# Attention on one core: the running maximum folded from 128 to 64 partitions ahead of its transposes

## The chip, the cores and the metric

The kernel runs on one core of a Trainium2 chip. A core has a matrix engine (TensorE, PE in the profile, with its weight loads as PEld), three engines for elementwise work (VectorE or DVE, ScalarE or ACT, GpSimd or POOL), and SyncE (SP), whose queue issues most of the transfers. Each engine works through its own list of instructions in order; between engines they wait for each other on semaphores. The metric is device time in microseconds for one execution of the whole layer.

## The reference, cut to what matters

One encoder layer with two groups of token mixers side by side: gated linear attention (group A) and multi-head latent attention (group B). Their outputs are concatenated, go through one output projection, and a LayerNorm of the scaled residual follows. The change touches the attention of group B alone:

```python
def attend(blk):
    qn, qr = blk
    s = (jnp.einsum('bqhd,bkhd->bhqk', qn, k_nope, preferred_element_type=jnp.float32)
         + jnp.einsum('bqhr,bkr->bhqk', qr, k_r, preferred_element_type=jnp.float32))
    p = jax.nn.softmax(s, axis=-1)
    return jnp.einsum('bhqk,bkhv->bqhv', p.astype(v.dtype), v)
```

There are 4 heads and 2048 positions; a softmax runs over all 2048 keys. It needs, for each query, the maximum of its scores over the keys, which is subtracted ahead of the exponential.

## The kernel before, in words

The kernel runs group A first, then the projections of group B, then from about 620 us on the attention, and last the output projection with its LayerNorm. Products are made to full precision by splitting each operand into a high and a low part, so one product is three matmuls (the helper at lines 419 to 423).

The attention (from line 1488) works in 16 blocks: 4 heads by 4 groups of 512 queries. Scores are held with **keys on the partitions and queries along the columns**. A block has 8 pairs of key tiles; a pair is 2 x 128 keys, and its scores fill a tile of 128 x 1024. For a pair, TensorE makes the scores (ten matmuls, tile pS, lines 1522 to 1526); ScalarE copies them to SBUF (s, line 1531); VectorE folds them into the running maximum (rm, 128 x 512, lines 1541 and 1544); later VectorE subtracts the block's maximum (line 1568), ScalarE takes the exponential (line 1572) and rounds its high part (ph, line 367), GpSimd takes the low part (pl, line 373), and TensorE multiplies by the values (o, six matmuls, lines 421 to 423). Sums of the exponentials run beside it: VectorE adds some pairs into ap (line 1595), GpSimd others into acc (lines 1598 and 1600).

After the last pair, rm still holds 128 partial maxima for each query, one on each partition. The kernel brings them together in three steps. In `tmax` TensorE transposes rm in four pieces of 128 columns into one PSUM bank (mx, line 1550). In `rmax` VectorE reduces each piece along its columns (mc, 128 x 4, line 1555). In `bmax` TensorE transposes each column of mc, spread over 128 columns, so that the maximum of each query stands on all partitions (mb, line 1562). Only then can the first subtraction of the block start.

The sums of the exponentials go a similar way at the block's end, in a form that the change takes up: ScalarE copies one half of the partitions onto the other (`own_half`, line 1627), VectorE adds the two halves (`fold`, line 1633), TensorE transposes two pieces instead of four (sx, line 1645), and VectorE reduces them over 256 columns (line 1654). Tiles mx, sx and the projected output y share one PSUM bank (tag x); y leaves it by a ScalarE copy (yc, line 1696).

The order of all engines is written out by hand. Each step gets a place, a number in units of one pair (tables `PLACE` from line 74, `PLACE_LAST` for the last block); all steps are sorted by it (line 1768) and every engine is held to that order (`in_order`, line 383):

```python
for i in range(nb):
    for j in range(NP):
        t = NP * i + j
        put(t, scores, i, j)
        ...
    for n, f in (("tmax", tmax), ("rmax", rmax), ("bmax", bmax)) + {nb - 1: (), nb - 2: own_late}.get(i, own):
        put(NP * i + NP - 1 + at(n, i), f, i)
```

So pair j of block i has place 8i + j for its scores, and a step of the table is counted from there; tmax, rmax and bmax are counted from the block's last pair, 8i + 7. The value products of pair 4 have 12.27 (`pv`), those of block i - 1 thus 8i + 8.27, or 1.27 when counted from block i's last pair. The running adds of line 1595, the sum's copies and folds, and the output steps are placed by the same tables.

Of the kernel before, what the change touches and what calls it, by code (L numbers as in the profile page):

```python
# [9 lines left out]
F32 = mybir.dt.float32  # L10
F32R = mybir.dt.float32r
I32 = mybir.dt.int32
AF = mybir.ActivationFunctionType
ALU = mybir.AluOpType
AX = mybir.AxisListType
# [3 lines left out]
P = 128  # L19
# [8 lines left out]
QB = 512  # L28
# [45 lines left out]
PLACE = dict(  # L74
    copy=0.73,
    max=1.21,
    sub=(9.47, 8.65, 7.39, 7.37, 7.49, 6.63, 6.95, 7.44),
    exp=(10.18, 9.95, 7.63, 9.15, 8.26, 9.12, 7.84, 8.01),
    hi=(10.39, 10.41, 9.81, 10.32, 9.82, 10.74, 10.53, 10.47),
    lo=(11.99, 11.22, 11.21, 12.62, 11.98, 11.51, 10.87, 10.63),  # L80
    pv=(12.35, 12.1, 11.89, 12.65, 12.27, 12.25, 12.14, 11.45),
    acc=(12.45, 11.78, 12.32, 0, 10.57, 11.24, 10.03, 9.22),
    acc0=10.78,
    tmax=1.26,
    rmax=1.27,
    bmax=1.48,
    tot=11.2,
    half=11.7,
    fold=11.95,
# [5 lines left out]
    y=16.55,  # L95
    yc=16.9,
)
PLACE_LAST = dict(
    sub=(9.67, 8.74, 8.38, 6.77, 10.45, 3.53, 9.53, 5.55),
    exp=(10.14, 9.35, 10.49, 8.31, 13.01, 14.59, 17.1, 18.05),  # L100
    hi=(10.43, 11.83, 12.21, 14.39, 15.18, 22.96, 28.7, 34.03),
# [255 lines left out]
class K:  # L357
# [1130 lines left out]
    def attention(self):  # L1488
        tc, nc = self.tc, self.nc
        mm = nc.tensor.matmul  # L1490
        V, G, Ac = nc.vector, nc.gpsimd, nc.scalar
        NP = NKT // 2
        with ExitStack() as ctx:
# [4 lines left out]
            pM, pO, pX, pA, pS = bank("pM"), bank("pO"), bank("pX"), bank("pA"), bank("pS", 2)  # L1498
            blocks = [(h, b) for b in range(NQB) for h in range(H)]
            nb = len(blocks)  # L1500
            stt = [dict(s=[None] * NP) for _ in blocks]
# [31 lines left out]
            def smax(i, j):  # L1533
# [8 lines left out]
                else:  # L1542
                    for e in range(2):
                        V.tensor_tensor(d["rm"], src[:, e], d["rm"], ALU.max)  # L1544

            def tmax(i):
                d = stt[i]
                d["x"] = pX.tile([P, 4, P], F32, tag="x", name=f"mx{i}")
                for e in range(4):
                    nc.tensor.transpose(d["x"][:, e], d["rm"][:, e * P:(e + 1) * P], self.ident)  # L1550

            def rmax(i):
                d = stt[i]
                d["mc"] = op.sm.tile([P, 4], F32, tag="mc", name=f"mc{i}")
                V.tensor_reduce(d["mc"], d["x"], AX.X, ALU.max)

            def bmax(i):

# [53 lines left out]
            def tot(i):  # L1612
# [4 lines left out]
                    return  # L1617
                for e in range(2):
                    V.tensor_tensor(d["ap"], d["ap"], d["as"][:, e], ALU.add)

            halves = [(slice(64 * e, 64 * e + 64), slice(64 - 64 * e, 128 - 64 * e), slice(e * QB // 2, (e + 1) * QB // 2))
                      for e in range(2)]

            def own_half(i):
                d = stt[i]
# [88 lines left out]
            def put(place, fn, *a):  # L1714
                todo.append((place, len(todo), fn, a))

            def at(f, i, j=None):
                p = PLACE_LAST.get(f, PLACE[f]) if i == nb - 1 else PLACE[f]
                return p[j] if isinstance(p, tuple) else p

            own = (("tot", tot), ("half", own_half), ("fold", fold), ("tsum", tsum), ("rcp", rcp), ("keep", keep), ("oh", oh), ("ol", ol), ("y", y), ("yc", yc))
            own_late = tuple(e for e in own if e[1] is not keep)
# [4 lines that stand above are left out]
                    for n, f in (("copy", copy), ("max", smax), ("sub", sub), ("exp", exp), ("hi", phi), ("lo", plo),  # L1727
                                 ("pv", pv), ("acc", acc)):
                        if n != "acc" or j != SUM_POOL[0] or i == nb - 1:
                            put(t + at(n, i, j), f, i, j)  # L1730
                put(NP * i + at("acc0", i), acc0, i)
                for n, f in (("tmax", tmax), ("rmax", rmax), ("bmax", bmax)) + {nb - 1: (), nb - 2: own_late}.get(i, own):
                    put(NP * i + NP - 1 + at(n, i), f, i)
                if i + 2 < nb:
                    put(NP * i + 4.05, fetch, i + 2)
# [295 lines left out]
```

## Time and profile before

| what | value |
|---|---|
| median of 3 runs | 1301.71 us (1299.26 to 1301.95) |
| profiled execution, own time | 1305.11 us |
| its span, first to last instruction | 1303.1 us |
| mean granted clock of TensorE | 0.997 |

In the profile's rows an engine is named by its letters, L and a number is a line of the kernel before, and "out<-in" names the tiles. A row of a timeline gives the start in us from the span's start, the duration, engine, line, operation and shapes; "x2" stands for two instructions that follow one another, and a bracket at the end gives the idle time of that engine just before, with what ended it. The ends of matmuls are modelled, and two matmuls overlap in the rows, so TensorE's pace is read from starts.

### The profile page before, as it was taken

What the parts mean: (1) busy time and instruction counts of PE and PEld (TensorE: products, weight loads), DVE (VectorE), ACT (ScalarE), POOL (GpSimd) and SP (SyncE); (2) the same over time, 40 slices, a digit from 0 to 9 for tenths busy, and PEclk for the clock granted to TensorE, in tenths of its full rate; (3) what the DMA queues carried; (4) which work ended last, traced back from release to release, by engine and by line L of the source; (5) the groups of instructions that cost most, each with busy time, mean ns of one, the idle gap of its engine ahead of it and who ended that gap; (6) DMA issues with size and microseconds to landing.
All of it is one profiled execution on the core that took longest, in us unless ns stands there. A gap on an engine that the chain in (4) does not pass through costs nothing.

```text
span 1303.1 us, 20008 instructions
## 1 busy us (share of the span) xinstructions
PE 1276.8 (98%) x7051; PEld 1126.2 (86%) x7051; DVE 970.7 (74%) x1742; ACT 821.2 (63%) x1369; POOL 783.8 (60%) x494
## 2 busy tenths in 40 slices
PE   7999999999999999999999999999999999999997
PEld 7999999999989999999788888888888887887886
DVE  7967774645675445555798888888888889486998
ACT  7764656655575565665688888888888888511110
POOL 0143333242448666672188888889999999934441
PEclk9999999999999999999999999999999999999999
DMA  8132313122475565555501111122223110375563
GB/s 285 62 101 54 94 49 91 56 68 79 131 241 170 190 216 192 179 193 170 163 1 41 41 41 41 41 57 60 63 78 100 43 41 9 122 237 169 198 199 111
DMA packets 107820, 145.82 MB, mean 112 GB/s; under 512 B 17250, under 2 KB 62694, under 8 KB 107720
## 3 DMA queue, kind: packets, MB, share of 16 engines
q1 hardware_dynamic: 99128, 142.41, 35.1%
q0 software_dynamic: 672, 2.10, 0.4%
q8 instruction: 56, 0.92, 0.3%
q10 hardware_dynamic: 7920, 0.03, 0.3%
q14 instruction: 44, 0.36, 0.1%
HBM read 94.14 MB, written 50.36 MB: 111 GB/s over the span
## 4 chain that ended last, share of the span: by engine, by line
PE 82%; DVE 4%; DMA 4%; ACT 3%; POOL 2%; issue 1%; SPq 0%; DVEq 0%; ACTq 0%; POOLq 0%
PE o L421 4%; PE o L422 4%; PE o L423 4%; PE pS L1522 4%; PE pS L1524 4%; PE pS L1523 4%; PE pS L1525 4%; PE pS L1526 4%; PE ipa L421 4%; PE ipa L423 4%; PE ipa L422 4%; PE pz L422 2%; PE pz L423 2%; PE pz L421 2%; PE ipg L421 2%; PE ipg L422 2%
## 5 line engine op out<-in xcount | busy, mean ns | idle before, releaser
L373 POOL TENSOR_TENSOR pl<-s,ph 128x1024 fp32r<-128x1024 f32 x128 | 306.1, 2414 | 55.8 <-ACT ph L367 55.8
L1544 DVE TENSOR_TENSOR rm<-pS,rm 128x512 f32<-128x512 f32 x210 | 144.8, 690 | 26.3 <-ACT s L1531 20.7
L1568 DVE TENSOR_TENSOR s<-s,mb 128x1024 f32<-128x1024 f32 x128 | 151.2, 1213 | 9.0 <-PE mb L1562 8.9
L1531 ACT ACTIVATE s<-pS 128x1024 f32<-128x1024 f32 x128 | 131.3, 1026 | 37.4 <-PE pS L1526 33.0
L1031 POOL TENSOR_TENSOR Us<-Us,cw 128x512 f32<-128x512 f32 x16 | 18.5, 1157 | 226.5 <-DVE Us L1029 174.7
L367 ACT ACTIVATE ph<-s 128x1024 fp32r<-128x1024 f32 x128 | 135.2, 1058 | 15.8 <-PE o L423 15.0
L1572 ACT ACTIVATE s<-s 128x1024 f32<-128x1024 f32 x128 | 131.5, 1051 | 13.4 <-DVE s L1568 13.3
L421 PE MATMUL ipa<-wah,xah 128*128 128x384 f32 (+1 forms) x384 | 130.5, 340 | 6.3 <-ACT wah L367 6.2
L422 PE MATMUL ipa<-wal,xah 128*128 128x384 f32 (+1 forms) x384 | 124.8, 325 | 0.1
L423 PE MATMUL ipa<-wah,xal 128*128 128x384 f32 (+1 forms) x384 | 124.9, 325 | 0.0
L1522 PE MATMUL pS<-qh,ckvT_h 128*128 128x512 f32 x256 | 102.6, 401 | 0.8 <-DVE rm L1544 0.4
L421 PE MATMUL o<-ph,vh 128*128 128x512 f32 x256 | 101.0, 395 | 0.0
L1525 PE MATMUL pS<-rh,krs 128*128 128x512 f32 x256 | 99.8, 390 | 0.0
L1523 PE MATMUL pS<-ql,ckvT_h 128*128 128x512 f32 x256 | 99.8, 390 | 0.0
L1524 PE MATMUL pS<-qh,ckvT_l 128*128 128x512 f32 x256 | 99.8, 390 | 0.0
L423 PE MATMUL o<-ph,vl 128*128 128x512 f32 x256 | 99.8, 390 | 0.0
L1526 PE MATMUL pS<-rl,krs 128*128 128x512 f32 x256 | 99.8, 390 | 0.0
L422 PE MATMUL o<-pl,vh 128*128 128x512 f32 x256 | 99.6, 389 | 0.0
L1595 DVE TENSOR_TENSOR ap<-ap,s 128x512 f32<-128x512 f32 x120 | 83.1, 693 | 3.5 <-ACT s L1572 0.7
L373 POOL TENSOR_TENSOR ol<-of,oh 128x512 fp32r<-128x512 f32 x32 | 42.9, 1343 | 66.2 <-ACT oh L367 65.4
L421 PEld LDWEIGHTS ipa<-wah,xah 128*128 128x128 f32 x384 | 73.2, 191 | 7.4 <-ACT wah L367 6.5
L421 PE MATMUL pz<-xch,wzh 128*128 128x256 f32 x256 | 74.8, 292 | 0.0
(327 smaller groups left out, 3874.7 us busy)
## 6 DMA issues: line engine op xcount, KB each, us to landing
xcf<-xT_dram SPq DMA_DIRECT2D x16, 512.0 KB, 5.2
xr<-x_dram SPq DMA_DIRECT2D x16, 512.0 KB, 6.3
out_dram<-rr SPq DMA_DIRECT2D x32, 256.0 KB, 2.1
xaf<-xT_dram SPq DMA_DIRECT2D x14, 512.0 KB, 4.3
oib<-oi_s SPq DMA_DIRECT2D x16, 256.0 KB, 4.2
qdb<-qd_s SPq DMA_DIRECT2D x16, 256.0 KB, 4.1
SU<-su_s SPq DMA_DIRECT2D x16, 256.0 KB, 4.5
ub<-u_s SPq DMA_DIRECT2D x16, 256.0 KB, 4.4
```

The source lines that it names most:

```text
L367: return nc.scalar.activation(dst, src, AF.Copy).ins
L373: return e.tensor_tensor(dst, src, hi.bitcast(F32), ALU.subtract).ins
L421: mm(out, ah, bh, start=start, stop=False)
L422: mm(out, ah, bl, start=False, stop=False)
L423: mm(out, al, bh, start=False, stop=stop)
L1522: mm(ps[:, e], kh, qh, start=True, stop=False)
L1523: mm(ps[:, e], kh, ql, start=False, stop=False)
L1524: mm(ps[:, e], kl, qh, start=False, stop=False)
L1525: mm(ps[:, e], kr, rh, start=False, stop=False)
L1526: mm(ps[:, e], kr, rl, start=False, stop=True)
L1544: V.tensor_tensor(d["rm"], src[:, e], d["rm"], ALU.max)
L1568: V.tensor_tensor(s, s, d["mb"][:, None, :].to_broadcast([P, 2, QB]), ALU.subtract)
```

## The change

In fourteen of the sixteen blocks (all but the first and the last), two steps come ahead of the transposes. In `other_half` ScalarE copies, for each half of the partitions, 256 columns of rm from the other half into the mx bank (two copies of 64 x 256, from SBUF to PSUM). In `fold_max` VectorE takes the maximum of these and the half's own 256 columns (two instructions of 64 x 256). After that the lower 64 partitions hold queries 0 to 255 and the upper 64 hold queries 256 to 511, each with 64 partial maxima, in 128 x 256. So `tmax` transposes two pieces instead of four, and `rmax` reduces 256 columns instead of 512, over 64 at a time. `bmax` is as before.

The places of the three old steps move in these blocks: tmax from 1.26 to 1.55, rmax from 1.27 to 1.56, bmax from 1.48 to 1.78. The new steps are at 1.22 and 1.23. The first and the last block keep the old steps and places.

```diff
@@ PLACE
-    tmax=1.26,
-    rmax=1.27,
-    bmax=1.48,
+    hmax=1.22,
+    fmax=1.23,
+    tmax=1.55,
+    rmax=1.56,
+    bmax=1.78,
...
+PLACE_FIRST = dict(
+    tmax=1.26,
+    rmax=1.27,
+    bmax=1.48,
+)
 PLACE_LAST = dict(
+    tmax=1.26,
+    rmax=1.27,
+    bmax=1.48,
...
+            halves = [(slice(64 * e, 64 * e + 64), slice(64 - 64 * e, 128 - 64 * e), slice(e * QB // 2, (e + 1) * QB // 2))
+                      for e in range(2)]
+
+            folded = lambda i: 0 < i < nb - 1
+
+            def other_half(i):
+                d = stt[i]
+                d["x"] = pX.tile([P, 4, P], F32, tag="x", name=f"mx{i}")
+                f = d["x"][:, 2:4].rearrange("p a t -> p (a t)")
+                for own_p, other_p, qs in halves:
+                    Ac.activation(f[own_p], d["rm"][other_p, qs], AF.Copy)
+
+            def fold_max(i):
+                d = stt[i]
+                f = d["x"][:, 2:4].rearrange("p a t -> p (a t)")
+                for own_p, _, qs in halves:
+                    V.tensor_tensor(d["rm"][own_p, :QB // 2], f[own_p], d["rm"][own_p, qs], ALU.max)
+
             def tmax(i):
                 d = stt[i]
-                d["x"] = pX.tile([P, 4, P], F32, tag="x", name=f"mx{i}")
-                for e in range(4):
+                if not folded(i):
+                    d["x"] = pX.tile([P, 4, P], F32, tag="x", name=f"mx{i}")
+                for e in range(2 if folded(i) else 4):
                     nc.tensor.transpose(d["x"][:, e], d["rm"][:, e * P:(e + 1) * P], self.ident)
 
             def rmax(i):
                 d = stt[i]
                 d["mc"] = op.sm.tile([P, 4], F32, tag="mc", name=f"mc{i}")
-                V.tensor_reduce(d["mc"], d["x"], AX.X, ALU.max)
+                if not folded(i):
+                    V.tensor_reduce(d["mc"], d["x"], AX.X, ALU.max)
+                else:
+                    V.tensor_reduce(d["mc"].rearrange("p (e j) -> p j e", e=2),
+                                    d["x"][:, 0:2].rearrange("p j (e k) -> p j e k", e=2), AX.X, ALU.max)
...
-                p = PLACE_LAST.get(f, PLACE[f]) if i == nb - 1 else PLACE[f]
+                p = PLACE_LAST.get(f, PLACE[f]) if i == nb - 1 else PLACE_FIRST.get(f, PLACE[f]) if i == 0 else PLACE[f]
...
-                for n, f in (("tmax", tmax), ("rmax", rmax), ("bmax", bmax)) + {nb - 1: (), nb - 2: own_late}.get(i, own):
+                fmax = (("hmax", other_half), ("fmax", fold_max)) if folded(i) else ()
+                for n, f in fmax + (("tmax", tmax), ("rmax", rmax), ("bmax", bmax)) + {nb - 1: (), nb - 2: own_late}.get(i, own):
                     put(NP * i + NP - 1 + at(n, i), f, i)
```

More of the change, by code (lines that the diff above doesn't have):

```diff
@@ L1619, in tot @@
                     V.tensor_tensor(d["ap"], d["ap"], d["as"][:, e], ALU.add)
-            halves = [(slice(64 * e, 64 * e + 64), slice(64 - 64 * e, 128 - 64 * e), slice(e * QB // 2, (e + 1) * QB // 2))
-                      for e in range(2)]
             def own_half(i):
```

## The prediction

> **What bounds the kernel now.** I read the page first (shares of busy time, the granted clock, the chain of waits), then the windows of the attention stage, its list of waits, and the timeline around one block boundary.
>
> ```profile
> PE 1276.8 (98%) x7051; PEld 1126.2 (86%) x7051; DVE 970.7 (74%) x1742; ACT 821.2 (63%) x1369; POOL 783.8 (60%) x494
> ...
> PEclk9999999999999999999999999999999999999999
> ...
> PE 82%; DVE 4%; DMA 4%; ACT 3%; POOL 2%; issue 1%; SPq 0%; DVEq 0%; ACTq 0%; POOLq 0%
> ```
>
> TensorE carries 82% of the chain that ends last, at a full granted clock. The change lies in the attention stage, from about 640 to 1098 us. Busy time in two windows, the second well inside that stage:
>
> ```profile
> 635.00:645.00 10.00, 8.91 (x43) 6.87 (x41) 8.43 (x12) 5.07 (x5) 0.00 (x0) 1.00 0.33 93
> 700.00:900.00 200.00, 200.00 (x914) 165.31 (x913) 179.87 (x250) 169.03 (x191) 169.41 (x72) 1.00 0.18 46
> ```
>
> PE (the first figure after the width) is busy 200.00 of 200 us; VectorE (third), ScalarE (fourth) and GpSimd (fifth) have 20 to 31 us free. From the list of waits of 640 to 1098 us (in total, times, longest):
>
> ```profile
> DVE mc L1555 <- PE mx L1550: 10.6, 14, 0.9
> PE mb L1562 <- DVE mc L1555: 0.8, 1, 0.8
> ```
>
> Today VectorE waits for the transposes of the maximum (14 times, 10.6 us together), and TensorE waits for the maximum only once, 0.8 us. So TensorE's own list sets the pace: a matmul taken from it is a gain, an idle gap in it is a loss, one for one. Boundary of block 3, TensorE's timeline (start, duration, instruction):
>
> ```profile
> 725.08 0.39 PE L1522 MATMUL pS<-qh,ckvT_h 128*128 128x512 f32 x1
> ...
> 727.12 0.39 PE L1526 MATMUL pS<-rl,krs 128*128 128x512 f32 x1
> 727.35 0.60 PE L1550 MATMUL mx<-ident,rm 128*128 128x128 f32 x4
> 727.70 0.48 PE L421 MATMUL o<-ph,vh 128*128 128x512 f32 x1
> 728.02 0.39 PE L422 MATMUL o<-pl,vh 128*128 128x512 f32 x1
> ...
> 729.16 0.60 PE L1562 MATMUL mb<-ident,mc 128*128 128x128 f32 x4
> 729.52 0.48 PE L1522 MATMUL pS<-qh,ckvT_h 128*128 128x512 f32 x1
> 729.83 0.39 PE L1523 MATMUL pS<-ql,ckvT_h 128*128 128x512 f32 x1
> ```
>
> Starts, not durations, tell the pace: nine steps from 725.08 to 727.12 are 0.227 us each. A group of four transposes takes 0.35 us to the next start, and that next matmul takes 0.32 instead of 0.227: 728.02 - 727.35 - 0.227 = 0.44 us for the mx group, and from 729.16 to 729.83 likewise 0.44 for mb. Both: 0.89 us a block. Between the two groups stand six matmuls of the probabilities by the values, and under them VectorE reduces the maximum:
>
> ```profile
> 724.36 1.42 DVE L1544 TENSOR_TENSOR rm<-pS,rm 128x512 f32<-128x512 f32 x2 [0.85 <-ACT s L1531]
> 725.69 1.42 DVE L1595 TENSOR_TENSOR ap<-ap,s 128x512 f32<-128x512 f32 x2
> 727.98 0.69 DVE L1555 TENSOR_REDUCE mc<-mx 128x4 f32<-128x512 f32 x1 [0.87 <-PE mx L1550]
> ...
> 729.87 3.48 DVE L1568 TENSOR_TENSOR s<-s,mb 128x1024 f32<-128x1024 f32 x3 [0.57 <-PE mb L1562]
> ```
>
> The reduction ends at 728.67 and mb goes at 729.16: 0.5 us to spare. **That cover is what the change moves.**
>
> **The change part by part.** *1. The order on TensorE.* tmax goes from place 1.26 to 1.55 and bmax from 1.48 to 1.78. The six o matmuls of pair 4 of the block before have place 1.27 on the same scale: they stood between mx and mb, and now stand ahead of mx. The changed list reads: ten score matmuls, six o matmuls, two mx, four mb, next scores. Nothing lies between mx and mb any more, so TensorE waits there through the whole reduction. Block 0 of this very trace has that order already, having no earlier block to fill the gap:
>
> ```profile
> 638.59 0.66 PE L1550 MATMUL mx<-ident,rm 128*128 128x128 f32 x4 [0.31 <-DVE rm L1544]
> 639.28 0.69 DVE L1555 TENSOR_REDUCE mc<-mx 128x4 f32<-128x512 f32 x1 [0.75 <-DMA rh<-rh_s]
> 640.03 0.65 PE L1562 MATMUL mb<-ident,mc 128*128 128x128 f32 x4 [0.79 <-DVE mc L1555]
> 640.43 0.48 PE L1522 MATMUL pS<-qh,ckvT_h 128*128 128x512 f32 x1
> 640.75 0.39 PE L1523 MATMUL pS<-ql,ckvT_h 128*128 128x512 f32 x1
> ```
>
> Four legs: first mx to reduction 0.69 (0.63 at block 3, where TensorE came in running); reduction 0.69; its end to mb 0.06; mb to the second score matmul 0.72.
>
> *2. What is cheaper.* Two mx transposes fewer, at 0.35 / 4 = 0.0875 us each: the first leg is 0.63 - 0.175 = 0.455 us. The reduction has 256 columns instead of 512. These group rows of the stage (660 to 1098 us: count, busy us, mean ns) hold its twin and those of the added work:
>
> ```profile
> L1633 DVE TENSOR_TENSOR acc<-ap,acc 64x256 f32<-64x256 f32 x28 | 11.8, 421 | 0.4
> L1627 ACT ACTIVATE acc<-ap 64x256 f32<-64x256 f32 x28 | 10.4, 371 | 0.2
> ...
> L1654 DVE TENSOR_REDUCE rc<-sx 128x4 f32<-128x256 f32 x14 | 5.8, 414 | 0.0
> ...
> L1587 ACT ACTIVATE ap<-s 128x512 f32<-128x512 f32 x14 | 8.4, 603 | 15.5 <-DVE acc L1633 15.5
> ```
>
> L1654 has the same form: 0.414 us. From the first mx to the second score matmul it is then 0.455 + 0.414 + 0.06 + 0.72 = 1.65 us, less 0.227 that the first score matmul takes anyhow: 1.42. (Of it 0.455 + 0.414 + 0.06 = 0.93 pass from the first mx to the first mb.) Against 0.89 today that is +0.54 us a block, in fourteen blocks **+7.5 us**. Without the wait, six transposes in one group would take 0.44 + 0.175 = 0.62, a gain of 0.27 a block or 3.7 us: the whole gain there is to have.
>
> The Trainium skill prices this otherwise. Its page "TensorE: Matmul & The Clock Gate", section "Back-to-back issue gap", gives about 81 ns for a weight load and matmul of 128 columns in a sustained stream; as an estimate from that page, eight transposes are 0.65 us instead of the 0.89 of the rows here. Today's groups would be cheaper by 0.24 and the last leg by about 0.17, and the sum 8.5 instead of 7.5. I take the rows, since the slow first matmul behind a group, 0.32, is in every one of them.
>
> *3. The added chain: ScalarE copies, VectorE folds.* Two copies 64x256 from SBUF into PSUM have no row. L1627, the same shape from PSUM to SBUF, takes 0.371; L1587, the same direction at four times the area, 0.603; L1696 below, 128x512 out of PSUM, 0.59, so the direction adds about 0.01. I take 0.39, nearest to L1627, with 0.36 and 0.60 as the ends. Two folds are L1633's form, 0.42 each. ScalarE at block 3:
>
> ```profile
> 723.30 1.03 ACT L1531 ACTIVATE s<-pS 128x1024 f32<-128x1024 f32 x1 [0.29 <-PE pS L1526]
> ...
> 725.17 0.59 ACT L1696 ACTIVATE yc<-y 128x512 f32<-128x512 f32 x1
> 725.64 1.06 ACT L367 ACTIVATE ph<-s 128x1024 fp32r<-128x1024 f32 x1
> 727.54 1.03 ACT L1531 ACTIVATE s<-pS 128x1024 f32<-128x1024 f32 x1 [0.84 <-PE pS L1526]
> 729.42 1.06 ACT L367 ACTIVATE ph<-s 128x1024 fp32r<-128x1024 f32 x1 [0.85 <-PE o L423]
> ```
>
> A hand-over takes 0.03 (s ends 724.33, rm starts 724.36). The copies stand behind yc, done at 725.76, and wait for rm, done at 725.78. Copies 0.78, folds 0.84, two hand-overs 0.06: the fold ends at 727.46. The moved mx starts six matmuls after 727.35, at 728.71, so it doesn't wait for the fold. But the two adds of L1595 are queued on VectorE between fold and reduction, 1.42 us: VectorE is free at 728.88, and mx lets the reduction start at 728.71 + 0.455 = 729.17. Slack 0.29: hidden. On ScalarE the ph behind the copies starts 0.95 late, and the idle 0.84 and 0.85 ahead of the next two instructions take it up. VectorE gets 0.84 - 0.28 = 0.56 us more a block, against (200 - 179.87) / 200, a tenth, of idle time: some 3 us a block. If that cover were gone, the 0.56 would come on top of the 0.54.
>
> Three blocks have their rm later against mx:
>
> ```profile
> 663.22 1.42 DVE L1544 TENSOR_TENSOR rm<-pS,rm 128x512 f32<-128x512 f32 x2 [0.85 <-ACT s L1531]
> 666.17 0.69 DVE L1555 TENSOR_REDUCE mc<-mx 128x4 f32<-128x512 f32 x1 [0.19 <-PE mx L1550]
> ...
> 1035.28 1.06 ACT L367 ACTIVATE ph<-s 128x1024 fp32r<-128x1024 f32 x1
> 1036.88 0.69 DVE L1555 TENSOR_REDUCE mc<-mx 128x4 f32<-128x512 f32 x1 [0.65 <-PE mx L1550]
> ...
> 1064.79 1.42 DVE L1544 TENSOR_TENSOR rm<-pS,rm 128x512 f32<-128x512 f32 x2 [0.95 <-ACT s L1531]
> 1067.76 0.69 DVE L1555 TENSOR_REDUCE mc<-mx 128x4 f32<-128x512 f32 x1 [0.22 <-PE mx L1550]
> ```
>
> mx allows the new reduction 1.36 - 0.175 = 1.19 us after the old start. Block 1: VectorE is free at 664.64 + 3.10 = 667.74, mx allows 667.36: 0.38 late. Block 14: 1069.31 against 1068.95: 0.36. In block 13 the copies stand behind another ScalarE copy (oh) and can't start before 1035.28: free at 1038.35 against 1038.07, 0.28. Together **+1.0 us**, paid by TensorE in the same gap.
>
> *4. DMAs and queues.* GpSimd's and SyncE's lists are unchanged; zero. First and last block keep their old places; zero.
>
> Sum: 7.5 + 1.0 = +8.6 us with the roundings. The profiled execution (1305.11 us, span 1303.1) becomes 1313.7; it lies 3.4 above the median of the runs. On the median: 1301.7 + 8.6 = **1310.3 us**.
>
> **The rivals.** *A, faster: the wait is hidden, the gain stays.* The place is the gap between mx and mb. It pays only if mb can follow the first mx within 0.93 - 0.54 = 0.39 us instead of 0.93, or if TensorE could make up the gap later. Then up to -3.7: 1298.0. For it: VectorE has time to spare. Against it: the leg to the reduction alone is 0.455, block 0 shows the wait, and 200.00 busy of 200 leaves nothing to make up with. *B, a longer wait: the copies are slow.* At 0.60 each the fold comes 0.42 later, 0.13 beyond the slack in eleven blocks and 0.42 in three: +2.7, 1313.0. For it: that slack is only 0.29. *C, the clock falls after each gap.* With the ten score matmuls of the next step at half rate, 10 x 0.227 a block: +32, 1342. Against it: block 0 idles longer, the granted clock of its window (635 to 645) is 1.00, and its matmuls follow at 0.32 and then at full rate. The page named above, "A second HAM failure mode: psum-queue depth-cycling", tells of such drops from frequent short idling between matmul groups. *D, no change:* the reduction starts early enough that gap and saved transposes cancel, 0.54 us a block earlier than the legs say: 1301.7. Against it: the legs are read from rows that agree with each other, 0.63 and 0.69 for the first.
>
> **How the numbers follow.** Forecast 0.74, B 0.14, A 0.05, D 0.04, C 0.03. The forecast's own spread, legs 0.1 us off a block (1.4 in fourteen), with the three late blocks or not (1.0) and runs from 1299.26 to 1301.95, gives 1306 to 1313; with B's bound and a run's spread on it, 1305.5 to 1314.5. Of a change, 0.2% (2.6 us) can be told from none: faster 0.05 (A), same 0.04 (D), slower 0.91 (the rest).
>
> **What would show it.** In the changed profile: PE waits for mc fourteen more times, about 0.6 us each by the profile's count from the end of the second mx (0.93 - 0.0875 - 0.27); mc at 0.41 us; folds 0.42 and copies near 0.39; VectorE no longer waits for mx in blocks 1, 13 and 14, with about 0.3 left in the others; the period of a block, now (1067.76 - 666.17) / 13 = 30.9 us, at about 31.4. Wrong if PE shows no new idle time there, if mx waits for the fold, or if other engines' waits take up the gap.

## The result, and the profile after

The changed kernel is slower: 1308.85 us (median of 5 runs, 1308.08 to 1311.96) against 1301.38 us for the kernel before (5 runs, 1299.26 to 1301.95), a ratio of 1.0065 with a 95% interval of 1.0051 to 1.008, or +7.5 us. The forecast was 1310.3 us, +8.6 us.

The boundary of block 3 in the changed kernel, TensorE's timeline (start, duration, engine, line, operation; lines are those of the changed kernel, where L1579 makes mx, L1595 mb, L1532 to L1536 the scores, L431 to L433 the value products):

```profile
728.44 0.39 PE L433 MATMUL o<-ph,vl 128*128 128x512 f32 x1
728.67 0.38 PE L1579 MATMUL mx<-ident,rm 128*128 128x128 f32 x2
729.57 0.65 PE L1595 MATMUL mb<-ident,mc 128*128 128x128 f32 x4 [0.52 <-DVE mc L1587]
729.97 0.47 PE L1532 MATMUL pS<-qh,ckvT_h 128*128 128x512 f32 x1
730.28 0.39 PE L1533 MATMUL pS<-ql,ckvT_h 128*128 128x512 f32 x1
```

The last value product is now ahead of mx, and between mx and mb TensorE stands still for 0.52 us by the profile's count, waiting for mc. From 728.67 to 730.28, less the 0.227 us of one matmul, are 1.38 us against the 0.89 of both groups before. VectorE and ScalarE at the same boundary (L1554 the running maximum, L1566 the copies, L1572 the folds, L1628 the two adds, L1587 the reduction, L1601 the subtractions):

```profile
724.32 1.42 DVE L1554 TENSOR_TENSOR rm<-pS,rm 128x512 f32<-128x512 f32 x2 [0.85 <-ACT s L1541]
726.66 0.86 DVE L1572 TENSOR_TENSOR rm<-mx,rm 64x256 f32<-64x256 f32 x2 [0.92 <-ACT mx L1566]
727.55 1.43 DVE L1628 TENSOR_TENSOR ap<-ap,s 128x512 f32<-128x512 f32 x2
729.09 0.42 DVE L1587 TENSOR_REDUCE mc<-mx 128x4 f32<-128x256 f32 x1
...
730.33 3.49 DVE L1601 TENSOR_TENSOR s<-s,mb 128x1024 f32<-128x1024 f32 x3 [0.21 <-PE mb L1595]
```

```profile
725.83 0.80 ACT L1566 ACTIVATE mx<-rm 64x256 f32<-64x256 f32 x2
```

The fold ends at 727.52, well ahead of mx; the adds end at 728.98, just ahead of the reduction. The list of waits of the attention stage (640 to 1106 us; in total, times, longest) has new rows, and a window of 200 us inside the stage shows what they take from TensorE (PE, the first figure after the width; the clock is the 1.00):

```profile
PEld mb L1595 <- DVE mc L1587: 11.7, 14, 1.3
PE mb L1595 <- DVE mc L1587: 8.4, 14, 1.1
```

```profile
700.00:900.00 200.00, 196.90 (x888) 161.66 (x887) 180.75 (x256) 170.19 (x200) 165.69 (x71) 1.00 0.17 45
```

TensorE's wait for mc comes fourteen times, 8.4 us together; before it came once, in block 0 (whose wait in the changed kernel lies just ahead of this window). And 196.90 us busy of 200 stand where 200.00 stood.

To compare kernels to a few hundredths of a microsecond a block, the period of a block serves better than the whole time: the starts of the reduction into mc in blocks 3 and 12, divided by nine. Of the kernel before and the changed one:

```profile
727.98 0.69 DVE L1555 TENSOR_REDUCE mc<-mx 128x4 f32<-128x512 f32 x1 [0.87 <-PE mx L1550]
...
1005.98 0.69 DVE L1555 TENSOR_REDUCE mc<-mx 128x4 f32<-128x512 f32 x1 [0.87 <-PE mx L1550]
```

```profile
1011.81 0.42 DVE L1587 TENSOR_REDUCE mc<-mx 128x4 f32<-128x256 f32 x1
```

(1005.98 - 727.98) / 9 = 30.89 us before, (1011.81 - 729.09) / 9 = 31.41 after: +0.52 us a block.

### The profile page after: what moved, and what is told of

Read it like the earlier page. It is cut to its first block, busy times and chain, and to the rows that moved or that the text cites. A ratio compares the mean times of both kernels' runs of the same rounds, so it can differ in the third digit from the quotient of the medians.

```text
span 1306.1 us, 20008 instructions
## 1 busy us (share of the span) xinstructions
PE 1274.1 (98%) x7023; PEld 1122.1 (86%) x7023; DVE 977.6 (75%) x1770; ACT 830.3 (64%) x1397; POOL 784.0 (60%) x494
## 4 chain that ended last, share of the span: by engine, by line
PE 77%; DVE 5%; POOL 4%; DMA 4%; ACT 3%; issue 2%; SPq 1%; DVEq 0%; POOLq 0%; ACTq 0%
PE pS L1532 4%; PE pS L1533 4%; PE pS L1536 4%; PE pS L1534 4%; PE pS L1535 4%; PE ipa L431 4%; PE o L431 4%; PE o L432 4%; PE o L433 4%; PE ipa L433 4%; PE ipa L432 4%; PE pz L432 2%; PE pz L433 2%; PE pz L431 2%; PE ipg L431 2%
## 5 line engine op out<-in xcount | busy, mean ns | idle before, releaser
L1554 DVE TENSOR_TENSOR rm<-pS,rm 128x512 f32<-128x512 f32 x210 | 144.8, 690 | 26.1 <-ACT s L1541 20.1
L1601 DVE TENSOR_TENSOR s<-s,mb 128x1024 f32<-128x1024 f32 x128 | 151.2, 1214 | 3.9 <-PE mb L1595 3.6
L431 PE MATMUL ipa<-wah,xah 128*128 128x384 f32 (+1 forms) x384 | 130.2, 339 | 6.8 <-ACT wah L377 6.7
L433 PE MATMUL ipa<-wah,xal 128*128 128x384 f32 (+1 forms) x384 | 124.8, 325 | 0.0
L1532 PE MATMUL pS<-qh,ckvT_h 128*128 128x512 f32 x256 | 102.5, 401 | 0.8 <-DVE rm L1554 0.4
L1536 PE MATMUL pS<-rl,krs 128*128 128x512 f32 x256 | 99.9, 390 | 0.0
L431 PE MATMUL o<-ph,vh 128*128 128x512 f32 x256 | 99.7, 390 | 0.0
L433 PE MATMUL o<-ph,vl 128*128 128x512 f32 x256 | 99.7, 389 | 0.0
L1628 DVE TENSOR_TENSOR ap<-ap,s 128x512 f32<-128x512 f32 x120 | 83.2, 693 | 3.8 <-ACT ap L1620 0.7
L431 PEld LDWEIGHTS ipa<-wah,xah 128*128 128x128 f32 x384 | 73.1, 190 | 7.8 <-ACT wah L377 7.0
L431 PE MATMUL pz<-xch,wzh 128*128 128x256 f32 x256 | 74.8, 292 | 0.0
```

What stands on the lines that cost most here:

```text
L431: mm(out, ah, bh, start=start, stop=False)
L433: mm(out, al, bh, start=False, stop=stop)
L1532: mm(ps[:, e], kh, qh, start=True, stop=False)
L1536: mm(ps[:, e], kr, rl, start=False, stop=True)
L1601: V.tensor_tensor(s, s, d["mb"][:, None, :].to_broadcast([P, 2, QB]), ALU.subtract)
```

## The experiments

The theory is the prediction's: the loss is TensorE's wait between mx and mb, because the moved places put the matmuls that covered the reduction ahead of mx. The main rival is that the added copies and folds cost the time, wherever mx stands. This table gathers the outcomes. The ratio is against the kernel before on the same chip; the period is worked out as above from the two starts given.

| kernel | ratio, 95% interval | reduction of block 3, of block 12 starts | period, us |
|---|---|---|---|
| before | 1 | 727.98, 1005.98 | 30.89 |
| changed | 1.0065 (1.0051 to 1.008) | 729.09, 1011.81 | 31.41 |
| places alone | 1.0107 (1.0089 to 1.0126) | 731.00, 1017.91 | 31.88 |
| fold, old places | 1.0065 (1.0049 to 1.0081) | 728.84, 1010.65 | 31.31 |
| mb later | 1.0164 (1.0146 to 1.0181) | 732.02, 1024.12 | 32.46 |
| reduction twice | 1.0114 (1.0093 to 1.0135) | 730.55, 1017.07 | 31.84 |
| one more copy | 1.011 (1.0094 to 1.0125) | 730.15, 1015.58 | 31.71 |
| adds moved | 1.0055 (1.004 to 1.007) | 728.32, 1010.60 | 31.36 |
| cover only | 1.0062 (1.0048 to 1.0075) | 730.31, 1012.19 | 31.32 |
| cover and adds | 1.0007 (0.9997 to 1.0018) | 728.69, 1006.42 | 30.86 |
| cover, cut at two | 0.9988 (0.9979 to 0.9997) | 726.61, 1002.74 | 30.68 |

### Places alone

```diff
-            folded = lambda i: 0 < i < nb - 1
+            folded = lambda i: False
```

> No folding: four transposes and the reduction over 512 columns as in the kernel before, only the three places moved (1.55, 1.56, 1.78) in the fourteen blocks. The theory (TensorE waits because no matmul stands between mx and mb any more): the legs of the prediction with four transposes and 0.69 us of reduction, 0.63 + 0.69 + 0.06 + 0.72 - 0.23 = 1.87 us a block against 0.89 before, +0.98, in fourteen blocks +13.7 us over the kernel before: about 1315 us, and TensorE waits for mc fourteen times. The rival (the added copies and folds cost the time): places alone cost nothing, about 1301 us.

The ratio is 1.0107, about +14 us, and the period +0.99 us, against +0.98 expected. No copy and no fold is in this kernel. TensorE at its boundary of block 3:

```profile
730.37 0.60 PE L1579 MATMUL mx<-ident,rm 128*128 128x128 f32 x4
731.75 0.65 PE L1595 MATMUL mb<-ident,mc 128*128 128x128 f32 x4 [0.79 <-DVE mc L1585]
```

The wait, 0.79 us, is the one that block 0 of the kernel before had already. So the places cost the time, and the folding gives back about half of it, 0.99 against 0.52 a block, by its smaller reduction and its two transposes less.

### The reduction twice

```diff
                 else:
-                    V.tensor_reduce(d["mc"].rearrange("p (e j) -> p j e", e=2),
-                                    d["x"][:, 0:2].rearrange("p j (e k) -> p j e k", e=2), AX.X, ALU.max)
+                    for _ in range(2):
+                        V.tensor_reduce(d["mc"].rearrange("p (e j) -> p j e", e=2),
+                                        d["x"][:, 0:2].rearrange("p j (e k) -> p j e k", e=2), AX.X, ALU.max)
```

> The changed kernel with the reduction into mc done twice in each of the fourteen blocks. The theory: the reduction lies whole on TensorE's path, so its second run adds 0.42 to 0.47 us a block, 6.0 to 6.6 us over the changed kernel: about 1315 us, and TensorE's wait for mc grows by as much. The rival (VectorE has time to spare there, the reduction is beside the path): about 1309 us.

The ratio is 1.0114, about 6.4 us above the changed kernel's 1.0065; the period rises from 31.41 to 31.84, +0.42. The extra reduction lands whole on TensorE's path: its wait for mc is now 15.0 us where it was 8.4.

```profile
PE mb L1596 <- DVE mc L1588: 15.0, 14, 1.6
```

### One more copy

```diff
                 for own_p, other_p, qs in halves:
                     Ac.activation(f[own_p], d["rm"][other_p, qs], AF.Copy)
+                own_p, other_p, qs = halves[1]
+                Ac.activation(f[own_p], d["rm"][other_p, qs], AF.Copy)
```

> The changed kernel with one of the two ScalarE copies of a block done once more, 0.38 us. It measures the slack that the prediction put at 0.29 us in eleven blocks (the trace of the changed kernel: the adds end at 728.89 when the next may start, the reduction starts at 729.09, so 0.20) and at none in three. The theory: 0.18 us in eleven blocks and 0.38 in three, +3.1 us over the changed kernel, 1312 us. If the copies are beside the path everywhere: +0, 1309 us. If they lie on it whole: 14 x 0.38 = +5.3 us, 1314 us.

More than expected: the ratio is 1.011, some 5.9 us above the changed kernel, and the period +0.30. VectorE's timeline in this kernel:

```profile
727.80 0.86 DVE L1574 TENSOR_TENSOR rm<-mx,rm 64x256 f32<-64x256 f32 x2 [1.34 <-ACT mx L1568]
728.69 1.43 DVE L1630 TENSOR_TENSOR ap<-ap,s 128x512 f32<-128x512 f32 x2
730.15 0.42 DVE L1589 TENSOR_REDUCE mc<-mx 128x4 f32<-128x256 f32 x1
```

VectorE waits for the copies 1.34 us instead of 0.92, so the fold is 0.42 later; 0.30 of that reaches the period. The times alone can't tell this from copies that lie on the path whole (+5.3 us expected there); the period can. The slack of the adds is 0.42 - 0.30 = 0.12 us, not 0.29. A copy that is off the path by 0.12 us is nearly on it.

### The adds moved

```diff
-                        if n != "acc" or j != SUM_POOL[0] or i == nb - 1:
+                        if n == "acc" and j == 5 and i < nb - 1:
+                            put(t + 11.205, acc, i, j, 0)
+                            put(t + 11.225, acc, i, j, 1)
+                        elif n != "acc" or j != SUM_POOL[0] or i == nb - 1:
                             put(t + at(n, i, j), f, i, j)
```

(`acc` takes a last argument that picks one of its two adds.)

> The changed kernel, its places as they are, with only the two adds of pair 5 taken from between fold and reduction. The theory: in the eleven regular blocks the reduction is set by mx, so the wait between mx and mb stays at 0.52 us; only the three blocks in which the adds held it back (waits of 1.06, 1.03 and 0.65 us in the trace) fall to 0.52: -1.2 us against the changed kernel, about 1308 us, too little for the times to show surely; TensorE's waits for mc go from 8.4 to about 7.3 us. If the adds set the wait in all blocks: the wait falls clearly below 0.5 us in each and the time by 3 us or more.

The wait at block 3 stays 0.52 us, and block 13, which had 1.03, falls to 0.52 as well, as block 1 and block 14 do:

```profile
728.80 0.65 PE L1595 MATMUL mb<-ident,mc 128*128 128x128 f32 x4 [0.52 <-DVE mc L1587]
...
1042.46 0.65 PE L1595 MATMUL mb<-ident,mc 128*128 128x128 f32 x4 [0.52 <-DVE mc L1587]
```

TensorE's waits for mc go from 8.4 to 7.2 us, as expected. The ratio, 1.0055, can't be told from the changed kernel's. The period is 0.05 shorter than the changed kernel's with the same wait; where that comes from is open.

### The fold with the old places

```diff
-    tmax=1.55,
-    rmax=1.56,
-    bmax=1.78,
+    tmax=1.26,
+    rmax=1.27,
+    bmax=1.48,
```

> The folding as changed, but tmax, rmax and bmax at their old places 1.26, 1.27 and 1.48, so that six matmuls stand between mx and mb again. The theory: mx now waits for the fold, about 0.25 us, and mb for the reduction, which is queued behind the two adds, about 0.2 us, against 0.27 us that the saved transposes give: +0.2 us a block, about +2.5 us over the kernel before (between +1 and +4), 1304 us. The rival (copies and folds cost the time wherever mx stands): as the changed kernel, about 1309 us.

By its time this looks like the rival: 1.0065, no better than the changed kernel, where 1304 us were expected. Its timeline tells another story (TensorE and VectorE at block 3):

```profile
726.48 0.86 DVE L1572 TENSOR_TENSOR rm<-mx,rm 64x256 f32<-64x256 f32 x2 [0.92 <-ACT mx L1566]
...
726.90 0.39 PE L1536 MATMUL pS<-rl,krs 128*128 128x512 f32 x1
727.37 1.43 DVE L1628 TENSOR_TENSOR ap<-ap,s 128x512 f32<-128x512 f32 x2
727.49 0.41 PE L1579 MATMUL mx<-ident,rm 128*128 128x128 f32 x2 [0.20 <-ACT ph L377]
727.65 0.48 PE L431 MATMUL o<-ph,vh 128*128 128x512 f32 x1
727.97 0.39 PE L432 MATMUL o<-pl,vh 128*128 128x512 f32 x1
...
728.84 0.42 DVE L1587 TENSOR_REDUCE mc<-mx 128x4 f32<-128x256 f32 x1
728.89 0.39 PE L433 MATMUL o<-ph,vl 128*128 128x512 f32 x1
729.32 0.65 PE L1595 MATMUL mb<-ident,mc 128*128 128x128 f32 x4
...
730.04 0.39 PE L1533 MATMUL pS<-ql,ckvT_h 128*128 128x512 f32 x1
```

mx could go at 726.90 + 0.23 = 727.13 and goes at 727.49: 0.36 us, of which the fold's end at 727.34 is 0.21 and the rest, 0.15, the hand-over. (The profile puts the wait down to ScalarE's ph, which ends at 727.43. But in block 15 of the kernel before, too, mx starts 0.14 us behind the end of the maximum that it waits for, 1096.60 against 1096.46.) The group of two costs 727.97 - 727.49 - 0.227 = 0.25 us, not the 0.44 - 0.175 = 0.27 assumed. mb could go at 729.12 and goes at 729.32, held by the reduction, which the adds hold: 0.20. And a mb that has waited takes 0.72 - 0.227 = 0.49 to the second score matmul, not 0.44. Together 0.36 + 0.25 + 0.20 + 0.49 = 1.30 against 0.89: +0.41, and the period says +0.42. So here, too, TensorE waits, at two places instead of one; the expected +0.2 was too low because 0.10 more of waiting for the fold, and the longer way out of a wait, were left out, and because the two transposes less save 0.19 a block in this place, not 0.27.

### mb later

```diff
-    bmax=1.78,
+    bmax=2.05,
```

> The changed kernel with bmax at 2.05 instead of 1.78: the ten score matmuls of the next pair stand between mx and mb. The theory: TensorE's wait for mc goes altogether; if nothing else comes in its place, -3.7 us against the kernel before, 1298 us. The subtractions start some 1.6 us later against TensorE, which VectorE's idle time (some 3 us a block) may not hold; then a wait for s, ph or pl shows up instead, and the time is up to 1304 us. The rival (copies and folds cost the time): about 1309 us still.

The wait for mc did go, as the theory has it: of TensorE's waits only the one of block 0 is left. But the kernel is the slowest of all, ratio 1.0164, about +21 us, where at most 1304 was expected. Rows of its list of waits, and VectorE's timeline at block 3:

```profile
DVE s L1601 <- PE mb L1595: 22.7, 14, 1.8
...
PE pS L1532 <- DVE rm L1554: 10.0, 15, 0.7
...
PE mb L1595 <- DVE mc L1585: 0.8, 1, 0.8
```

```profile
732.37 0.68 DVE L1551 TENSOR_TENSOR rm<-pS,s 128x512 f32<-128x512 f32 x1
734.82 3.48 DVE L1601 TENSOR_TENSOR s<-s,mb 128x1024 f32<-128x1024 f32 x3 [1.77 <-PE mb L1595]
738.22 1.43 DVE L1652 TENSOR_TENSOR ap<-ap,acc 128x512 f32<-128x512 f32 x2
739.55 1.41 DVE L1554 TENSOR_TENSOR rm<-pS,rm 128x512 f32<-128x512 f32 x2
```

VectorE now stands still 1.77 us for mb, then has the three subtractions and everything queued behind them, the running maxima of the next pairs too. Those release the score tiles (two of them), and TensorE waits for them: 10.0 us on pS. As these rows read, VectorE's 3 us of idle time a block can't be spent at this place, since its order is fixed and the work that would fill the gap stands behind the subtraction; no run with another order of VectorE tested that.

### Cover only, and cover with the adds moved

Both give six matmuls back to the wait, cut one and five around mx, so that the fold has one matmul more to finish. The second also moves the adds, as in the diff above.

```diff
-    tmax=1.55,
-    rmax=1.56,
-    bmax=1.78,
+    tmax=1.28,
+    rmax=1.281,
+    bmax=1.48,
...
+                pv_part(i, j, 0, cut if j == 4 and i < nb - 1 else 6)
+
+            def pv_part(i, j, a, b):
+                d = stt[i]
+                for w, v, start, stop in d["pv", j][a:b]:
+                    mm(d["o"], w, v, start=start, stop=stop)
...
+            cut = 1
...
+                if i < nb - 1:
+                    put(NP * i + 4 + at("pv", i, 4) + 0.02, pv_part, i, 4, cut, 6)
```

> As the kernel with the cover given back (matmuls cut one and five around mx), but with the two adds left between fold and reduction. The theory: mx doesn't wait, but the adds hold the reduction back until about 0.35 us after mb could go: 0.35 - 0.27 = +0.1 us a block, +1 us over the kernel before, 1302.5 us (1301 to 1304), and TensorE waits for mc by 0.3 to 0.4 us a block. If the adds don't matter: as with the adds moved, 1298 us.

> The folding as changed, with cover given back: the six matmuls of pair 4 of the block before are cut one and five, mx stands behind the first, mb behind the last; and the two adds of pair 5 leave the place between fold and reduction, one going ahead of the last pair's maxima, the other ahead of the fold, where VectorE waits for ScalarE's copies. The theory: mx starts about 0.1 us after the fold's end, the reduction ends half a microsecond ahead of mb, TensorE waits for neither, and the saved transposes stay: up to -3.7 us against the kernel before, 1297.7 us. If the copies and folds cost time by themselves: 1304 us or more.

With the adds in place the ratio is 1.0062 and the period +0.43, against +0.1 expected: the reduction waits for the adds, and mb for it, at block 3 until 730.79, 0.41 us after the last of the six matmuls lets it go. So the cover alone gives back only 0.09 of the 0.52 us a block.

```profile
728.85 1.44 DVE L1628 TENSOR_TENSOR ap<-ap,s 128x512 f32<-128x512 f32 x2
730.31 0.42 DVE L1587 TENSOR_REDUCE mc<-mx 128x4 f32<-128x256 f32 x1
```

With the adds moved the same order on TensorE gives 1.0007 (0.9997 to 1.0018) and a period of 30.86: the whole loss is gone, with every copy and fold still there (L1650 makes the value products in this kernel and the next).

```profile
727.88 0.39 PE L1650 MATMUL o<-ph,vh 128*128 128x512 f32 x1
728.25 0.41 PE L1579 MATMUL mx<-ident,rm 128*128 128x128 f32 x2
...
728.69 0.42 DVE L1587 TENSOR_REDUCE mc<-mx 128x4 f32<-128x256 f32 x1 [0.59 <-PE mx L1579]
728.73 0.40 PE L1650 MATMUL o<-ph,vl 128*128 128x512 f32 x1
...
729.66 0.60 PE L1595 MATMUL mb<-ident,mc 128*128 128x128 f32 x4
```

That refutes the rival: copies and folds cost nothing by themselves. They cost where mx or the reduction stands too close behind them, as with the old places. Of the hoped-for -3.7 us nothing came, though, because mx started 0.14 us later than TensorE could have taken it (it goes 0.15 us after the fold's end at 728.10), and a group of two costs 728.73 - 728.25 - 0.227 = 0.25 us there, so that it saves only 0.19.

### Cut at two

```diff
-            cut = 1
+            cut = 2
```

> As the kernel with cover and moved adds, but the six matmuls cut two and four around mx. There mx still started 0.14 us later than TensorE could have taken it (0.12 us after the fold's end), and a group of two transposes cost 0.25 us against 0.44 for four, so that 0.19 saved and 0.14 lost made about nothing. One matmul more ahead of mx (0.23 us) covers the 0.14; behind it four matmuls (0.91 us and the 0.25 of the group) still cover the reduction, which needs 0.42 + 0.42 + 0.06 us. The theory: -0.19 us a block against the kernel before, -2.6 us or ratio 0.998. If something else holds the block's period: no change, ratio 1.000 to 1.001.

```profile
726.20 0.38 PE L1579 MATMUL mx<-ident,rm 128*128 128x128 f32 x2
726.33 0.48 PE L1650 MATMUL o<-ph,vl 128*128 128x512 f32 x1
726.65 0.40 PE L1650 MATMUL o<-ph,vh 128*128 128x512 f32 x1
...
727.35 0.60 PE L1595 MATMUL mb<-ident,mc 128*128 128x128 f32 x4
...
1033.55 0.41 PE L1579 MATMUL mx<-ident,rm 128*128 128x128 f32 x2 [0.39 <-ACT ph L377]
```

In the eleven regular blocks neither mx nor mb waits any more, TensorE is busy 200.00 of 200 us again from 700 to 900, and the period is 30.68: -0.21 a block, -0.19 expected. In blocks 1, 13 and 14, whose rm comes late, mx still waits for the fold: it starts 0.75, 0.77 and 0.38 us behind the matmul ahead of it instead of 0.23, 1.2 us more together, and the expectation left that out. So 14 x 0.21 - 1.2 = 1.7 us are left of the gain, and the time agrees: 1300.44 us against 1302.19 beside it, a ratio of 0.9988 (0.9979 to 0.9997). This version beats both kernels, the one before only by the little that two transposes are worth.

## Why the prediction was right

**The bound.** TensorE's list set the pace, and an idle gap in it cost one for one. The doubled reduction shows it most plainly: 0.42 us more there, 0.42 us more of period.

**The order (step 1).** The predicted gap of TensorE, about 0.6 us (0.93 - 0.0875 - 0.27 = 0.57), was measured as 0.52 in the eleven regular blocks. Places alone measured +0.99 a block, where the same legs with four transposes gave +0.98.

**The legs (step 2).** Predicted +0.54 a block, measured +0.52 by the period; the rows of block 3 give 1.38 - 0.89 = +0.49, and the 0.03 between is not in them. First mx to reduction 729.09 - 728.67 = 0.42 (0.455 assumed), reduction 0.42 (0.414), its end to mb 0.06 (0.06), mb to the second score matmul 0.71 (0.72). The estimate from the Trainium skill's page "TensorE: Matmul & The Clock Gate", section "Back-to-back issue gap", would have made the sum 0.61 a block. The trace doesn't agree with that page's 81 ns: a transpose costs 0.11 us here, as the paragraph on the gain shows.

**The added chain (step 3).** Copies 0.38 each (0.39), folds 0.42 (0.42), and the fold ended at 727.52 in the trace, 1.15 us ahead of mx: hidden, as said. The slack of the adds was mis-sized: 0.12 instead of 0.29. The copies start 0.09 us behind rm (725.83 against 725.74) instead of 0.03, a pair takes 0.80 instead of 0.78 and the two folds 0.86 instead of 0.84, the adds start 0.03 after the fold's end, and mx lets the reduction start 0.42 us after it instead of 0.455. So the line that VectorE would still wait for mx by about 0.3 us in eleven blocks was wrong: only about 0.1 us is left, and the list of waits shows none. The sum did not hang on it, but it was close: one copy more cost 0.30 a block. For the same reason rival B was nearer than its place in the prediction makes it look.

**The three late blocks.** Predicted 0.38, 0.28 and 0.36 us for blocks 1, 13 and 14; the rows of TensorE's timeline give gaps of 1.06, 1.03 and 0.65 against 0.52:

```profile
666.83 0.65 PE L1595 MATMUL mb<-ident,mc 128*128 128x128 f32 x4 [1.06 <-DVE mc L1587]
...
1044.21 0.65 PE L1595 MATMUL mb<-ident,mc 128*128 128x128 f32 x4 [1.03 <-DVE mc L1587]
...
1075.73 0.65 PE L1595 MATMUL mb<-ident,mc 128*128 128x128 f32 x4 [0.65 <-DVE mc L1587]
```

That is 0.54, 0.51 and 0.13 more, together 1.2 for the predicted 1.0. The cause was right: with the adds moved all three fall to 0.52. The sizes were not: two came out higher by 0.2 and one lower by 0.2, so that their sum is near is in part luck.

**The sum.** 14 x 0.52 + 1.2 = 8.5 us by the trace, 8.6 predicted, and 7.5 by the medians, whose interval reaches from 6.6 to 10.4.

**The gain that did not come.** The prediction put the whole of it at 0.27 a block. Without any wait it is 0.21. The term that was off is the price of a transpose, 0.35 / 4 = 0.0875, with the slow matmul behind a group as a cost of its own. A group of two, where nothing waits, costs 726.65 - 726.20 - 0.227 = 0.22 us (cut at two), and the trace before had one in every block, the two transposes of sx:

```profile
740.52 0.38 PE L1645 MATMUL sx<-ident,acc 128*128 128x128 f32 x2
...
740.97 0.39 PE L1523 MATMUL pS<-ql,ckvT_h 128*128 128x512 f32 x1
```

That is 0.45 - 0.227 = 0.22 again, half of the 0.44 of four: 0.11 us a transpose, and nothing for the group as such. So two transposes less are worth 0.22, wherever they stand. With that price the first leg is 0.63 - 0.22 = 0.41, and the prediction's way from mx to the second score matmul becomes 0.41 + 0.414 + 0.06 + 0.72 - 0.227 = 1.38 us, as measured, instead of 1.42.

**Rivals.** A (hidden, 1298.0) and D (no change) fell with the measured wait. B's slow copies did not come, 0.38 us each, though the slack that it counted on was smaller than said there. C, a clock that drops after each gap, did not happen: the clock of the window from 700 to 900 us is 1.00 with a gap in each block, and the score matmuls behind a gap come at 0.31 us and then 0.23.

## What to carry to other kernels

Where one engine's list sets the pace and two of its steps have another engine's answer between them, count what stands between the two, in time, against the whole answer: the engine's own latency, the hand-overs, and what is queued ahead of the answer on the other engine. A change that makes both steps cheaper still loses if it moves the cover away. Here two things had to be put right at once: the cover back alone gave 0.09 us a block, the adds out of the way alone 0.05, both together 0.55. And work that is beside the path by only a tenth of a microsecond should be costed as if it were on it.

## What the runs showed that was not expected

Cover can be too long: ten matmuls between mx and mb instead of six removed the wait and cost 21 us. By its waits, the fixed order of VectorE turned a later subtraction into late maxima and these into late score tiles.

Two transposes in a group cost 0.22 us where nothing waits (0.25 where the first one waited) and four 0.44, so a transpose costs 0.11 us. The first 512-column matmul behind a group takes 0.31 to 0.32 us to the next start instead of 0.227, whatever the group's size, but the group's own steps are short by as much, 0.13 for two and 0.35 for four. The price is read from the group's start to the second matmul behind it.

A pair of folds whose two halves start on different partitions takes 0.86 us for two instructions of 0.42, and the adds start 0.03 us after its end, while the adds start 0.09 us before the reported end of a pair of maxima (725.69 against 725.78 in the kernel before).
